# Row sums of 16,384 rows: the last row's partial sum carried as an element, waits put into no-ops, pieces of 576 and 448

## Chip, cores and metric

One core of a Trainium2 chip. The metric is the device time of one execution in microseconds (us). The traces' records are in nanoseconds (ns). Where a time is given to 1 ns, it is the trace's own record of that instruction or of that load's semaphore; the views round to 10 ns.

## What is computed

```python
def setup_inputs():
    batch, seq, dim = 32, 512, 1024
    return {"x": np.random.randn(batch, seq, dim).astype(np.float32)}

def reference(x):
    return np.sum(x, axis=-1).astype(np.float32)
```

That is 16,384 sums of 1024 floats: 67 MB in, 64 KB out.

## The kernel before

Each of 128 partitions gets 128 rows. They arrive in loads of 16 rows into three buffers, and the DVE (VectorE) reduces them. Each load is issued while earlier ones are still under way, so that the stream does not stop (418 GB/s over the span). The last 16 rows come in smaller loads (9, 4 and 2 rows, then row 15 in two pieces), so that little is left to sum when the last byte lands. ACT (ScalarE) sums some of those rows, and seven of each partition's rows in the load before.

```python
CUT = 544
...
    part = rpool.tile([P, 1], F32, name="part")
    seen = rpool.tile([P, 1], F32, name="seen")
...
    def pairs_dve(xt, a, b, first, acc, pairs):      # one custom DVE op: sum over both halves of a piece
        h = (a + b) // 2
        nc.vector.tensor_tensor_reduce(
            out=pairs[:, 0 : h - a], in0=xt[:, a:h], in1=xt[:, h:b], scale=1.0, scalar=first,
            op0=ADD, op1=ADD, accum_out=acc,
        )
...
    cuts = [0, 9, 13, 15]
    ...                                               # loads of rows 0-8, 9-12, 13-14
    last = 15 * D
    for i, k in ((0, CUT), (CUT, D)):
        nc.sync.dma_start(
            out=xt[:, last + i : last + k],
            in_=x_b[:, c * D + last + i : c * D + last + k],
        )
    ...                                               # rows 0-12 between DVE and ACT
    pairs_dve(xt, 13 * D, 14 * D, 0.0, res[:, c + 13 : c + 14], pairs[2])
    rows_act(xt, res, 14, 1, c + 14)
    pairs_dve(xt, last, last + CUT, 0.0, part, pairs[0])              # piece one

    nc.vector.tensor_copy(out=seen, in_=part)
    pairs_dve(xt, last + CUT, last + D, part, res[:, c + 15 : c + 16], pairs[1])   # piece two
    nc.sync.dma_start(out=out_b, in_=res)
```

The copy is there for its wait. Piece two needs two things: its own load, and the sum of piece one, which it takes as a start value from memory (`part`). In the built program such an instruction carries one wait. The copy waits for the sum; piece two, behind it, waits for the load. Each custom op is followed by a second instruction that reads out the accumulator (80 to 84 ns in the trace of before) and raises the DVE's semaphore.

Of the kernel before, what the change touches and what calls it, by code (L numbers as in the profile page):

```python
# [1 line left out]

# [4 lines left out]

F32 = mybir.dt.float32
ADD = mybir.AluOpType.add
COPY = mybir.ActivationFunctionType.Copy  # L10
X = mybir.AxisListType.X

BLOCKS = (112, 16)
G = 16
ACT_ROWS = 7
CUT = 544
EARLY = 2


@with_exitstack  # L20
def row_sums(
    ctx: ExitStack,
    tc: tile.TileContext,
    x: bass.AP,
    out: bass.AP,
):
    nc = tc.nc
    P = nc.NUM_PARTITIONS

    x_flat = x.flatten_outer_dims()  # L30
    R, D = x_flat.shape
    C = R // P
    assert R % P == 0 and sum(BLOCKS) == C
    out_flat = out.rearrange("a (b c) -> (a b c)", c=1)

    xpool = ctx.enter_context(tc.tile_pool(name="x", bufs=3))
    rpool = ctx.enter_context(tc.tile_pool(name="res", bufs=1))
    part = rpool.tile([P, 1], F32, name="part")
    seen = rpool.tile([P, 1], F32, name="seen")
    pairs = [rpool.tile([P, D // 2], F32, name=f"pairs{i}") for i in range(3)]  # L40

    def rows_dve(xt, res, j, n, c):
        nc.vector.tensor_reduce(  # L43
            out=res[:, c : c + n],
            in_=xt[:, j * D : (j + n) * D].rearrange("p (j d) -> p j d", d=D),
            axis=X,
            op=ADD,
        )

    def sum_act(v, acc):  # L50
        nc.scalar.activation(out=v, in_=v, func=COPY, accum_out=acc)  # L51

    def rows_act(xt, res, j, n, c):
        for i in range(n):
            sum_act(xt[:, (j + i) * D : (j + i + 1) * D], res[:, c + i : c + i + 1])

    def pairs_dve(xt, a, b, first, acc, pairs):
        h = (a + b) // 2
        nc.vector.tensor_tensor_reduce(  # L59
            out=pairs[:, 0 : h - a], in0=xt[:, a:h], in1=xt[:, h:b], scale=1.0, scalar=first,  # L60
            op0=ADD, op1=ADD, accum_out=acc,
        )

    def block(r0, n):
        x_b = x_flat[r0 : r0 + P * n].rearrange("(p c) d -> p (c d)", p=P)
        out_b = out_flat[r0 : r0 + P * n].rearrange("(p c) -> p c", p=P)
        return x_b, out_b, rpool.tile([P, n], F32, name=f"res{r0}")

    full = C - G
    done = 0  # L70
    for b, n in enumerate(BLOCKS):
        x_b, out_b, res = block(done * P, n)
        final = b == len(BLOCKS) - 1
        whole = n - G if final else n
        c = 0
        while c < whole:
            m = min(G, whole - c)
            xt = xpool.tile([P, G * D], F32, tag="xt", name="xt")
            parts = (0, 1, m) if done + c == 0 else (0, m)
            for i, k in zip(parts, parts[1:]):  # L80
                nc.sync.dma_start(
                    out=xt[:, i * D : k * D], in_=x_b[:, (c + i) * D : (c + k) * D]
                )
            a = ACT_ROWS if done + c + m == full else 0
            rows_dve(xt, res, 0, m - a, c)
            rows_act(xt, res, m - a, a, c + m - a)
            c += m
        if not final:

            for i, k in ((0, 104), (104, P)):  # L90
                nc.scalar.dma_start(out=out_b[i:k], in_=res[i:k])
        done += n

    xt = xpool.tile([P, G * D], F32, tag="xt", name="xt")
    cuts = [0, 9, 13, 15]
    for i, k in zip(cuts, cuts[1:]):
        nc.sync.dma_start(out=xt[:, i * D : k * D], in_=x_b[:, (c + i) * D : (c + k) * D])  # L97
    last = 15 * D
    for i, k in ((0, CUT), (CUT, D)):
        nc.sync.dma_start(  # L100
            out=xt[:, last + i : last + k],
            in_=x_b[:, c * D + last + i : c * D + last + k],
        )

    for i, k in zip(cuts[:2], cuts[1:3]):
        h = (k - i) // 2
        rows_dve(xt, res, i, h, c + i)
        rows_act(xt, res, i + h, k - i - h, c + i + h)
    pairs_dve(xt, 13 * D, 14 * D, 0.0, res[:, c + 13 : c + 14], pairs[2])
    rows_act(xt, res, 14, 1, c + 14)  # L110
    pairs_dve(xt, last, last + CUT, 0.0, part, pairs[0])


    nc.vector.tensor_copy(out=seen, in_=part)  # L114
    pairs_dve(xt, last + CUT, last + D, part, res[:, c + 15 : c + 16], pairs[1])
    nc.sync.dma_start(out=out_b, in_=res)


def kernel(tc: tile.TileContext, x: bass.AP, out: bass.AP):
    row_sums(tc, x, out)  # L120
    tc.close()
    tc.compile()  # L122



    sp = mybir.EngineType.SP
    fn = tc.nc.m.functions[0]
    entry, body = None, None
    for blk in fn.blocks:
        ops = [i for i in blk.instructions if i.engine == sp]  # L130
        if entry is None:
            entry = blk
        elif any(i.opcode == "DMACopy" for i in ops):
            body = blk
            break
    code = list(body.instructions)
    loads = [i for i in code if i.engine == sp][:EARLY]
    for load in loads:
        assert load.opcode == "DMACopy" and not load.sync_info.on_wait
        code.remove(load)  # L140
    body.instructions = code
    code = list(entry.instructions)
    at = next(k for k, i in enumerate(code) if i.engine == sp and i.opcode == "Drain")
    code[at:at] = loads
    entry.instructions = code

# [1 line left out]
_INS = ['x']  # L148
_OUTS = [((32, 512), 'float32')]


# [23 lines left out]
```

## Time and profile before

| | before |
|---|---|
| median of all its fast runs up to the result | 162.02 us (161.98 to 162.34, 6 runs) |
| span in the trace | 160.59 us |
| HBM rate over the span | 418 GB/s |
| last load's landing to the store's start | 563 ns |
| store's start to the end of the span | 2.23 us |

The prediction starts from 162.18 us, which is the median of three runs (162.02 to 162.34). It shows the page and the end of the timeline. In a timeline line stand the start (us), the length (us), engine, source line, operation, output<-input and their shapes; in brackets at the end, idle time before it and what ended it. An operation "before" another can overlap it, since the next op of the same engine starts ahead of the recorded end (piece one 74 ns before the end of row 13's op, piece two 54 ns before the end of the copy). The one view that it speaks of and does not show is the chain of waits, the pieces of work that ended last (start, length, what):

```profile
157.32 0.36 DVE pairs L59
157.68 0.02 DVE part L59
157.73 0.15 DVE seen L114
157.88 0.41 DVE pairs L59
```

In it the copy (`seen`) seems to be worth 0.15 us. The chain follows each instruction back to one releaser, and if an engine was never idle it goes back along the engine. A load that landed under the copy does not appear in it.

### The profile page before, as it was taken

The numbers are of one execution on the slowest core, as the hardware profiler recorded it, in microseconds if no ns is written. First come the engines' busy times: TensorE is split into PE (matmuls) and PEld (weight loads), VectorE is DVE, ScalarE is ACT, GpSimd is POOL, SyncE is SP. The second block draws the span as 40 slices with busy tenths as digits, with TensorE's granted clock in tenths as the row PEclk, the third lists the DMA queues.
The fourth block names the chain that finished last, engine by engine and source line by source line (L and its number), as shares of the span: only waits on it lengthen the run. The fifth ranks groups of instructions, "written<-read, shape, count | busy, mean of one in ns | idle before, by whom it ended". The sixth has DMA issues, their size and how long they took to land.

```text
span 160.6 us, 120 instructions
## 1 busy us (share of the span) xinstructions
DVE 121.4 (76%) x16; ACT 17.2 (11%) x31; POOL 0.2 (0%) x4
## 2 busy tenths in 40 slices
DVE  0000059997799958999499994999949999598884
ACT  0000000000000000000000000000000000596892
POOL 0000000000000000000000000000000000000000
DMA  9997996996996996996996979979969969998991
GB/s 375 490 398 337 490 522 294 490 522 261 522 506 278 522 506 278 522 506 278 522 506 278 522 326 457 522 310 473 522 294 490 522 261 522 432 432 369 410 402 62
DMA packets 2169, 67.18 MB, mean 418 GB/s; under 512 B 505, under 2 KB 633, under 8 KB 889
## 3 DMA queue, kind: packets, MB, share of 16 engines
q1 hardware_dynamic: 2016, 67.12, 97.2%
q10 hardware_dynamic: 153, 0.06, 0.1%
HBM read 67.11 MB, written 0.07 MB: 418 GB/s over the span
## 4 chain that ended last, share of the span: by engine, by line
DMA 75%; DVE 22%; SPq 0%; issue 0%; DVEq 0%
DMA xt<-in_x_dram 75%; DVE res L43 21%; DVE pairs L59 1%; SPq L97 0%; DVE seen L114 0%; DVE part L59 0%; DVEq L122 0%; DVE res L59 0%
## 5 line engine op out<-in xcount | busy, mean ns | idle before, releaser
L43 DVE TENSOR_REDUCE res<-xt 128x16 f32<-128x16384 f32 (+3 forms) x9 | 119.8, 13309 | 36.6 <-DMA xt<-in_x_dram 36.6
L51 ACT ACT_TABLE_LOAD x1 | 1.3, 1283 | 138.3 <-DMA xt<-in_x_dram 138.3
L51 ACT ACTIVATE xt<-xt 128x1024 f32<-128x1024 f32 x15 | 15.6, 1042 | 2.2 <-DMA xt<-in_x_dram 2.2
L51 ACT ACTIVATION_READ_ACCUMULATOR xt<-xt 128x1 f32 x15 | 2.8, 186 | 0.0
L59 DVE CUSTOM_DVE_ANT_0 pairs<-xt 128x512 f32<-128x512 f32 (+1 forms) x2 | 1.1, 566 | 0.3 <-DMA xt<-in_x_dram 0.3
L59 DVE CUSTOM_DVE_ANT_0 pairs<-xt,part 128x240 f32<-128x240 f32 x1 | 0.5, 467 | 0.0
L114 DVE COPY seen<-part 128x1 f32<-128x1 f32 x1 | 0.2, 153 | 0.0
L59 DVE DVE_READ_ACCUMULATOR2_ANT res<- 128x1 f32 x2 | 0.2, 81 | 0.0
L159 POOL MEMSET const-bfloat16-1.0<- 128x1 bf16 x1 | 0.1, 101 | 0.0
L159 POOL MEMSET const-uint8-127<- 128x1 uint8 x1 | 0.1, 101 | 0.0
L159 POOL MEMSET const-float32-0.0<- 128x1 f32 x1 | 0.1, 98 | 0.2 <-issue 0.2
L159 POOL MEMSET const-float32-1.0<- 128x1 f32 x1 | 0.1, 98 | 0.0
L59 DVE DVE_READ_ACCUMULATOR2_ANT part<- 128x1 f32 x1 | 0.1, 84 | 0.0
## 6 DMA issues: line engine op xcount, KB each, us to landing
xt<-in_x_dram SPq DMA_DIRECT2D x1, 7680.0 KB
xt<-in_x_dram SPq DMA_DIRECT2D x1, 4608.0 KB, 32.4
xt<-in_x_dram SPq DMA_DIRECT2D x1, 2048.0 KB, 36.9
xt<-in_x_dram SPq DMA_DIRECT2D x1, 1024.0 KB, 39.0
xt<-in_x_dram SPq DMA_DIRECT2D x1, 512.0 KB, 3.9
xt<-in_x_dram SPq DMA_DIRECT2D x1, 272.0 KB, 39.1
xt<-in_x_dram SPq DMA_DIRECT2D x1, 240.0 KB, 38.9
xt<-in_x_dram SPq DMA_DIRECT2D x6, 40.9
```

The lines of the kernel that those rows point to most:

```text
L43: nc.vector.tensor_reduce(out=res[:, c : c + n], in_=xt[:, j * D : (j + n) * D].rearrange("p (j d) -> p j d", d=D), axis=X, op=ADD,)
L51: nc.scalar.activation(out=v, in_=v, func=COPY, accum_out=acc)
L59: nc.vector.tensor_tensor_reduce(out=pairs[:, 0 : h - a], in0=xt[:, a:h], in1=xt[:, h:b], scale=1.0, scalar=first, op0=ADD, op1=ADD, accum ...
L114: nc.vector.tensor_copy(out=seen, in_=part)
L159: nc = _bacc.Bacc("TRN2", target_bir_lowering=False, num_devices=1)
```

## The change

The intent: drop the copy, drop the start value from memory, and take the extra wait off the store. A gap of 16 columns is left between the pieces; the partial sum is written into the last but one of them, just ahead of piece two, with a zero beside it, so that one op over 450 elements (partial sum, zero and the 448 of piece two) gives the row's sum. The waits that the ops need besides their own are put into no-ops ahead of them. The cut moves, to make piece two, which is summed after the last landing, shorter.

```diff
-CUT = 544
+CUT = 576
...
-    part = rpool.tile([P, 1], F32, name="part")
-    seen = rpool.tile([P, 1], F32, name="seen")
+    tail = rpool.tile([P, D + 16], F32, name="tail")
+    part, zero = tail[:, CUT + 14 : CUT + 15], tail[:, CUT + 15 : CUT + 16]
+    blank = nc.vector.memset(zero, 0.0)
...
-    def pairs_dve(xt, a, b, first, acc, pairs):
+    def pairs_dve(v, a, b, acc, pairs):
...                                        # scalar=first becomes scalar=0.0
-    for i, k in ((0, CUT), (CUT, D)):
+    for i, k, gap in ((0, CUT, 0), (CUT, D, 16)):
         nc.sync.dma_start(
-            out=xt[:, last + i : last + k],
+            out=tail[:, i + gap : k + gap],
...
-    pairs_dve(xt, last, last + CUT, 0.0, part, pairs[0])
+    carry = pairs_dve(tail, 0, CUT, part, pairs[0])
-    nc.vector.tensor_copy(out=seen, in_=part)
-    pairs_dve(xt, last + CUT, last + D, part, res[:, c + 15 : c + 16], pairs[1])
-    nc.sync.dma_start(out=out_b, in_=res)
+    tc.keep_in_program_order(nc.vector.keepalive_nop([nc.vector.lower_ap(tail[:, CUT + 14 : CUT + 16])]))
+    total = pairs_dve(tail, CUT + 14, D + 16, res[:, c + 15 : c + 16], pairs[1])
+    for i in (blank, carry):
+        tc.declare_no_dep(total.ins, i.ins, reason="the wait is in the nop before it")
+    tc.keep_in_program_order(nc.sync.keepalive_nop([nc.sync.lower_ap(res[:, c + 14 : c + 15])]))
+    store = nc.sync.dma_start(out=out_b, in_=res)
+    for i in by_act:                       # ScalarE's sums
+        tc.declare_no_dep(store.ins, i.ins, reason="the wait is in the nop before it")
```

In the built program a no-op is a semaphore instruction of the engine's queue: it waits for one semaphore and raises another, which the program waits for at its end (21 ns long on the DVE's queue and 17 on the store's, in the trace of the changed kernel).

More of the change, by code (lines that the diff above doesn't have):

```diff
@@ L50, in sum_act @@
     def sum_act(v, acc):
-        nc.scalar.activation(out=v, in_=v, func=COPY, accum_out=acc)
+        return nc.scalar.activation(out=v, in_=v, func=COPY, accum_out=acc)
+    by_act = []
     def rows_act(xt, res, j, n, c):
         for i in range(n):
-            sum_act(xt[:, (j + i) * D : (j + i + 1) * D], res[:, c + i : c + i + 1])
-    def pairs_dve(xt, a, b, first, acc, pairs):
+            by_act.append(
+                sum_act(xt[:, (j + i) * D : (j + i + 1) * D], res[:, c + i : c + i + 1])
+            )
+    def pairs_dve(v, a, b, acc, pairs):
         h = (a + b) // 2
-        nc.vector.tensor_tensor_reduce(
-            out=pairs[:, 0 : h - a], in0=xt[:, a:h], in1=xt[:, h:b], scale=1.0, scalar=first,
+        return nc.vector.tensor_tensor_reduce(
+            out=pairs[:, 0 : h - a], in0=v[:, a:h], in1=v[:, h:b], scale=1.0, scalar=0.0,
             op0=ADD, op1=ADD, accum_out=acc,
@@ L98, in row_sums @@
     last = 15 * D
-    for i, k in ((0, CUT), (CUT, D)):
+    for i, k, gap in ((0, CUT, 0), (CUT, D, 16)):
         nc.sync.dma_start(
-            out=xt[:, last + i : last + k],
+            out=tail[:, i + gap : k + gap],
             in_=x_b[:, c * D + last + i : c * D + last + k],
         )
+    by_act.clear()
     for i, k in zip(cuts[:2], cuts[1:3]):
@@ L108, in row_sums @@
         rows_act(xt, res, i + h, k - i - h, c + i + h)
-    pairs_dve(xt, 13 * D, 14 * D, 0.0, res[:, c + 13 : c + 14], pairs[2])
+    pairs_dve(xt, 13 * D, 14 * D, res[:, c + 13 : c + 14], pairs[2])
     rows_act(xt, res, 14, 1, c + 14)
-    pairs_dve(xt, last, last + CUT, 0.0, part, pairs[0])
-    nc.vector.tensor_copy(out=seen, in_=part)
-    pairs_dve(xt, last + CUT, last + D, part, res[:, c + 15 : c + 16], pairs[1])
-    nc.sync.dma_start(out=out_b, in_=res)
+    carry = pairs_dve(tail, 0, CUT, part, pairs[0])
[7 more added lines that the diff above has]
+        tc.declare_no_dep(store.ins, i.ins, reason="the wait is in the nop before it")
 def kernel(tc: tile.TileContext, x: bass.AP, out: bass.AP):
```

## The prediction

The working of two terms was not taken from the traces: 392 ns for piece two's op (step 2, where the gain of 75 is 467 - 392) and 457 for piece one's (step 3, from 157.28 to 157.737). The sum is left as it came out: -75 + 24 - 36, so a gain of 87 ns and 162.09 us. For the two terms an estimate: without a start value the custom op took 692 ns at 512 pairs and 441 at 272 in the trace of before, which is 1.046 ns for each pair between them, and a straight line through the two has 392 at 225 pairs, 458 at 288 and some 407 at 240. The op with a start value took 467 at 240 pairs, so some 60 over the line; the prediction left open whether they came from the start value in memory or from the start inside the copy's last 54 ns.

> **What bounds the kernel now.** I read the page first (shares, slices, chain), then the timeline of the last five microseconds, then the waits of the two last loads, then the issue queue's own waits. From the page of the kernel before:
>
> ```profile
> span 160.6 us, 120 instructions
> DMA  9997996996996996996996979979969969998991
> HBM read 67.11 MB, written 0.07 MB: 418 GB/s over the span
> DMA 75%; DVE 22%; SPq 0%; issue 0%; DVEq 0%
> ```
>
> The loads run from the first slice to the 39th of 40; the chain is 75% load, and the DVE's 22% in it are two reductions that a later load was issued behind, in the middle of the stream. The change touches none of that: same bytes, same order, same issue waits. It can act only behind the last bytes. That stretch, in the timeline:
>
> ```profile
> 156.62 0.69 DVE L59 CUSTOM_DVE_ANT_0 pairs<-xt 128x512 f32<-128x512 f32 x1 [0.26 <-DMA xt<-in_x_dram]
> 157.24 0.44 DVE L59 CUSTOM_DVE_ANT_0 pairs<-xt 128x272 f32<-128x272 f32 x1
> 157.59 0.19 ACT L51 ACTIVATION_READ_ACCUMULATOR xt<-xt 128x1 f32 x1
> 157.61 0.08 DVE L59 DVE_READ_ACCUMULATOR2_ANT part<- 128x1 f32 x1
> 157.73 0.15 DVE L114 COPY seen<-part 128x1 f32<-128x1 f32 x1
> 157.82 0.47 DVE L59 CUSTOM_DVE_ANT_0 pairs<-xt,part 128x240 f32<-128x240 f32 x1
> 158.22 0.08 DVE L59 DVE_READ_ACCUMULATOR2_ANT res<- 128x1 f32 x1
> 158.36 0.35 SPq L116 DMA_DIRECT2D out_dram<-res  x1
> ```
>
> To be seen: the end is a row of DVE work (piece one, copy, piece two), then the store at 158.36. From there to the end of the span, 160.59, are 2.23 us: 1.4 from issue to landing of the store, and the closing barrier. The change has nothing in those.
>
> The chain of waits lists the copy as a link, but it cannot show a landing that ends just after it. So I looked at the issue and landing of the last two loads (source line 100):
>
> ```profile
> 118.12 1.12 SPq L100 DMA_DIRECT2D xt<-in_x_dram  x2
> L100 SPq DMA_DIRECT2D xt<-in_x_dram x2: 328/382/437, 118.1 to 118.9; - x2
> DMA to landing us min/median/max: 38.9/39.0/39.1
> ```
>
> Piece one: 118.12 + 39.1 = 157.22. Piece two is issued at 118.12 + 1.12 - 0.33 = 118.91 and lands 38.9 later, at 157.81; the landing records of the same trace have 157.80 for its sixteenth increment. The DVE's piece two starts at 157.825, some 24 ns behind the landing, which is the same delay that a load elsewhere shows (landing 41.325, reduction 41.348). So **piece two starts on its data, not on the copy**. By the DVE's own order it could have started at about 157.805: the op of piece one starts 74 ns before the op ahead of it ends (156.62 + 0.69 against 157.24), and the copy ends at 157.88. The copy costs at most nothing to speak of in the time.
>
> The store's wait, from the view of its line and from the first reduction's:
>
> ```profile
> L116 SPq EVENT_SEMAPHORE  x1: 20068/20068/20068, 138.3 to 138.3; - x1
> L43 DVEq EVENT_SEMAPHORE  x1: 21/21/21, 22.0 to 22.0; - x1
> ```
>
> The first waits from 138.27 to 158.33 for the DVE's last sum (semaphore record 158.311), and only then the store starts, at 158.364: 53 ns behind the semaphore. A load on the same queue that waits for the DVE by itself starts 17 ns behind it (39.307 to 39.324; 116.778 to 116.795). The second is a wait on the DVE's own queue: landing 21.977, wait 22.006 to 22.027, reduction at 22.076, so 99 ns where a direct wait takes 23.
>
> [...]here the last 1920-byte packet ends at 157.376 and the landing is 0.43 us later, so moving the cut moves bytes between pieces but hardly the last landing.
>
> **The change, part by part.**
>
> 1. Copy gone. It held piece two back by nothing (157.805 against 157.825). Gain 0. The memset of one column at the start of the DVE's queue lies in its 22 us of waiting for the first load: cost 0.
>
> 2. Piece two without a scalar operand, and shorter. It now takes 448 elements, the partial sum and a zero: 450, as 225 pairs. [...]Gain 75 ns, on the path.
>
> 3. Piece one longer, 576 elements as 288 pairs: [...]32 elements x 4 B x 128 = 16 KB more to land first. The landings of the two pieces are 584 ns apart for 246 KB, so 16 KB take 39 ns: landing 157.256 instead of 157.217. It starts 24 later at 157.28 (before 157.243), ends at 157.737, and its semaphore comes 19 behind that, as in before (157.684 to 157.703): 157.756. The last landing stays at 157.80, for the sum of bytes is the same (the packets take 88 and 79 ns; scaled, 93 and 74, the same sum).
>
> 4. The no-op on the DVE's queue. In the built program it is a semaphore instruction that waits for piece one's sum, and piece two behind it waits for its load alone. If it behaves as the one at 22.0 us: 23 from semaphore to wait, 21 long, 49 to the next op. So piece two may start at 157.756 + 0.093 = 157.849. Its data allow 157.825. The no-op then binds, by 24 ns. Loss 24 ns, on the path, in exchange for the copy.
>
> 5. The no-op on the store's queue. In the built program the ScalarE wait and the old store's wait stand in two semaphore instructions, both long fulfilled (ScalarE ends at 157.78), and the store waits for the DVE alone. 53 becomes 17: gain 36 ns, on the path.
>
> Sum: 157.849 + 0.392 = 158.241, semaphore 158.260, store 158.277 against 158.364. **Gain 87 ns**, which is -75 + 24 - 36. From there the end is the same 2.23 us. 162.18 - 0.09 = **162.09 us**, -0.05%.
>
> **The rivals.**
>
> *All the savings in series.* If the copy did gate piece two, its removal would start it right behind piece one: with the no-op free, at 157.73 instead of 157.82, and the whole would be 0.10 + 0.075 + 0.036 = 0.21 us, so 161.97. For it speaks the chain, which names the copy; against it the landing at 157.80.
>
> *The landing stays the gate and the no-op is free.* Then piece two starts at 157.825, gain 111 ns, 162.07. [...]the 49 ns at 22.0 us were seen with all else fulfilled.
>
> *The cut has moved too far.* Piece one, its sum and the no-op now come in one row behind a later landing. Every ns that the first landing slips beyond 157.256 goes to the end: at 100 ns the gain is gone, 162.19. The landings of one load spread by 0.39 us from first to sixteenth, but the last one alone counts, and it came 0.11 us behind the fifteenth in both pieces. Nothing in the trace says that this grows.
>
> *The 225-pair op is slow for its odd starts* (its second operand begins at an odd element). No op in the trace shows this, it would cost at most the 75 ns of step 2, and the end would be 162.17.
>
> **Range and chances.** The rivals span 161.97 to 162.19, less than what single runs of the same kernel do: 162.02 to 162.34, 0.32 us. So the range is set by the scatter of the stream's 160 us and not by the change: 161.80 to 162.40. A gain of 2% would need 3.2 us; all the work behind the last byte before the store is about 1.1 us, so faster has 1%. Slower by 2% would need a disturbance of the load stream, whose issue order and waits are unchanged: 1%. Within 2%: 98%.
>
> **What would show it right or wrong.** The timeline after should show: no copy; piece one at 157.28 for 0.46, piece two 0.10 to 0.13 behind its end in place of right on its landing, for 0.39 and not 0.47; the store some 36 ns behind the final accumulator's end (17 behind its semaphore) instead of 72. If the 225-pair op takes 0.45, step 2 is wrong and the scalar was not the cost. If piece two starts within 30 ns of its landing with the no-op done earlier, step 4 is wrong. If the last load lands elsewhere than 0.58 us or less behind the first piece, step 3 is. Times must be taken from the last landing, since the stream itself shifts by tenths of a microsecond between runs. The whole is wrong if the load stream's rate changes: then the mean of 418 GB/s on the page would move.

## The result

162.16 us in the median (161.95 to 162.34, 6 runs) against 162.02 us (161.98 to 162.34, 6 runs) before. The ratio of the two is 1.0003, with a 95% interval of 0.999 to 1.0016. (A ratio is the mean time of one kernel's runs over that of the other's of the same rounds, so not quite the ratio of the medians.) The interval is some 0.2 us to either side; neither a gain of 0.09 us nor none can be told from it. The traces can say more. The page of the changed kernel, for the stream:

```profile
span 160.3 us, 122 instructions
DMA  9997997996996996996996996996998999998991
HBM read 67.11 MB, written 0.07 MB: 419 GB/s over the span
```

The stream is as it was: 419 GB/s against 418. The span is 0.27 us shorter, but that is where the loads happened to end in this execution: the last landing is at 157.537 against 157.801. So times have to be taken from landings. The timeline of the end:

```profile
156.39 0.69 DVE L66 CUSTOM_DVE_ANT_0 pairs<-xt 128x512 f32<-128x512 f32 x1 [0.34 <-DMA xt<-in_x_dram]
157.01 0.46 DVE L66 CUSTOM_DVE_ANT_0 pairs<-tail 128x288 f32<-128x288 f32 x1
157.39 0.08 DVE L66 DVE_READ_ACCUMULATOR2_ANT tail<- 128x1 f32 x1
157.66 0.40 DVE L66 CUSTOM_DVE_ANT_0 pairs<-tail 128x225 f32<-128x225 f32 x1 [0.19 <-DMA tail<-in_x_dram]
157.97 0.08 DVE L66 DVE_READ_ACCUMULATOR2_ANT res<- 128x1 f32 x1
158.09 0.35 SPq L129 DMA_DIRECT2D out_dram<-res  x1
```

The no-ops are not in the timeline, as semaphore instructions are not counted as work. The view of the first one's source line has it, and the view of the last two loads has their landings:

```profile
L122 DVEq EVENT_SEMAPHORE  x1: 21/21/21, 157.5 to 157.5; - x1
```

```profile
L107 SPq DMA_DIRECT2D tail<-in_x_dram x2: 328/387/446, 117.7 to 118.4; - x2
DMA to landing us min/median/max: 39.2/39.3/39.3
```

What to see: the copy is gone and piece two is 0.40 long in place of 0.47, as intended. But the DVE now stands idle for 0.19 us before it. The bracket puts that down to the load, which landed at 157.537 (118.36 + 39.2); yet the op began only at 157.656, 119 ns behind the landing, where a landing by itself is followed by its op in 24 ns. The no-op ran from 157.509 to 157.530. It is what stood between, and no view names it: the releaser is the semaphore that came last, and that was the load's, 7 ns behind the no-op's end. From the last landing to the store's start are 549 ns, 14 less than before.

### The profile page after: what moved, and what is told of

Read it like the earlier page. It is cut to its first block, busy times and chain, and to the rows that moved or that the text cites. A ratio compares the mean times of both kernels' runs of the same rounds, so it can differ in the third digit from the quotient of the medians.

```text
span 160.3 us, 122 instructions
## 1 busy us (share of the span) xinstructions
DVE 121.3 (76%) x16; ACT 17.2 (11%) x31; POOL 0.2 (0%) x4
## 4 chain that ended last, share of the span: by engine, by line
DMA 75%; DVE 22%; another core or an unknown queue 1%; issue 0%; DVEq 0%
DMA xt<-in_x_dram 50%; DMA tail<-in_x_dram 24%; DVE res L46 21%; DVE pairs L66 0%; DVEq L137 0%
## 5 line engine op out<-in xcount | busy, mean ns | idle before, releaser
L66 DVE CUSTOM_DVE_ANT_0 pairs<-tail 128x288 f32<-128x288 f32 (+1 forms) x2 | 0.9, 426 | 0.2 <-DMA tail<-in_x_dram 0.2
L66 DVE CUSTOM_DVE_ANT_0 pairs<-xt 128x512 f32<-128x512 f32 x1 | 0.7, 692 | 0.3 <-DMA xt<-in_x_dram 0.3
## 6 DMA issues: line engine op xcount, KB each, us to landing
xt<-in_x_dram SPq DMA_DIRECT2D x1, 1024.0 KB, 39.2
tail<-in_x_dram SPq DMA_DIRECT2D x1, 224.0 KB, 39.2
```

The source lines that it names most:

```text
L66: return nc.vector.tensor_tensor_reduce(out=pairs[:, 0 : h - a], in0=v[:, a:h], in1=v[:, h:b], scale=1.0, scalar=0.0, op0=ADD, op1=ADD, ac ...
```

## The experiments

Ten runs were made: seven edited kernels, then three kernels timed in five rounds. The question was why the op behind the no-op starts 126 ns after the no-op's end, where the prediction had 49, taken from the only other wait on the DVE's queue in front of an op. Theory U: the no-op's raising of a semaphore holds what comes next (the wait with 49 raises none). Theory C: the custom op takes long to begin behind a wait that stands by itself on the queue (the op with 49 behind its wait is a plain reduction). The first four runs take the two apart. The seven kernels that were given one look have a single time each, 162.15 to 162.68 us, which tells nothing at this size.

### The wait without the raising

```diff
-    tc.keep_in_program_order(nc.vector.keepalive_nop([...]))
     total = pairs_dve(tail, CUT + 14, D + 16, res[:, c + 15 : c + 16], pairs[1])
-    for i in (blank, carry):
-        tc.declare_no_dep(total.ins, i.ins, reason="the wait is in the nop before it")
```

> The changed kernel without the no-op on the DVE's queue. The built program then puts the landing's wait into a semaphore instruction that raises nothing, and the last pair op waits for piece one's sum itself, which is long there. In the changed kernel the op began 126 ns after the end of its no-op, where 49 were predicted. Theory U (it is the no-op's own raising of a semaphore that holds the next instruction): here, without one, the op begins about 49 ns after the end of the wait, some 100 ns after the last landing, and the store starts about 530 ns after the last landing. Theory C (this custom op takes long from the sequencer to the engine[...]): again about 126 ns after the end of the wait, 175 ns after the last landing, and the store about 600 ns after it.

The last landing was at 158.095. From the view of the last op's source line, then from the timeline:

```profile
L66 DVEq EVENT_SEMAPHORE  x1: 21/21/21, 158.1 to 158.1; - x1
```

```profile
158.23 0.40 DVE L66 CUSTOM_DVE_ANT_0 pairs<-tail 128x225 f32<-128x225 f32 x1 [0.21 <-DMA tail<-in_x_dram]
```

The wait began 28 ns after the landing and ended at 49, the op began at 134: 85 ns behind the wait. That is neither 49 nor 126 but the middle, and so is the store, 562 ns behind the last landing. Neither theory alone holds.

### A plain reduction behind the no-op

```diff
-    total = pairs_dve(tail, CUT + 14, D + 16, res[:, c + 15 : c + 16], pairs[1])
+    total = nc.vector.tensor_reduce(
+        out=res[:, c + 15 : c + 16], in_=tail[:, CUT + 14 : D + 16], axis=X, op=ADD
+    )
```

> The changed kernel with its no-op, but the last sum is a plain reduction of the same 450 elements in place of the custom pair op. Theory U (the no-op's raising of a semaphore costs): the reduction begins 126 ns after the end of the no-op, as the pair op did. Theory C (the custom op's own way from sequencer to engine costs): it begins about 49 ns after the no-op, as the first reduction of the program does behind its wait, or, where the landing is later than that allows, some 24 ns after the landing.[...]

```profile
157.47 0.08 DVE L66 DVE_READ_ACCUMULATOR2_ANT tail<- 128x1 f32 x1
157.70 0.62 DVE L123 TENSOR_REDUCE res<-tail 128x1 f32<-128x450 f32 x1
```

The no-op's record is 157.595 to 157.616, so the reduction began 85 ns behind it, again the middle. It is 622 long. An estimate from the program's other reductions comes to the same (2,286 ns for 2,048 elements and 17,220 for 16,384 in the trace of before: 1.042 ns for each element between them, and 153 besides). The four cases together:

| ns from the wait's end to the op's start | reduction behind it | custom op behind it |
|---|---|---|
| wait that raises nothing | 49 to 50 (first reduction of every trace) | 85 |
| no-op that raises a semaphore | 85 | 126 |

The four cases fit both theories together, with 35 to 41 ns each. They differ in more than the two: the waits of the upper row are for a load and those of the lower for a sum, and the first reduction comes after 22 us of idle time. The next run bears on the first of these: the op stands 127 ns behind a no-op that waits for nothing. The second is not tested. What in the hardware takes these times is not shown.

### Two no-ops

```diff
+    tc.keep_in_program_order(nc.vector.keepalive_nop([...]))      # a second time
```

> The changed kernel with a second no-op, which waits for nothing, behind the first on the DVE's queue. It raises its semaphore too. Theory U: each no-op that raises a semaphore costs the next instruction the same, so the pair op begins 126 + 21 + some 120 ns after the end of the first. Theory C: the second costs only its own step in the sequencer, 40 to 70 ns, and the pair op begins 126 ns after the end of the second, so 170 to 220 ns after the end of the first.

```profile
L123 DVEq EVENT_SEMAPHORE  x1: 21/21/21, 157.8 to 157.8; - x1
```

```profile
157.99 0.40 DVE L66 CUSTOM_DVE_ANT_0 pairs<-tail 128x225 f32<-128x225 f32 x1 [0.28 <-DMA tail<-in_x_dram]
```

The first no-op ended 19 ns before the last landing; the second (the line above) ran from 57 to 78 ns after it, and the op began at 205: 127 behind the second. So the second one cost 76 + 21 = 97 ns, more than theory C's 40 to 70 and less than the 141 of theory U, although it waits for nothing. The store started 635 ns behind the last landing, 86 later than in the changed kernel, whose no-op ended 12 ns later against the landing.

### The copy in place of the DVE's no-op

```diff
...                                        # the tile seen is made again
-    tc.keep_in_program_order(nc.vector.keepalive_nop([...]))
+    nc.vector.tensor_copy(out=seen, in_=part)
     total = pairs_dve(tail, CUT + 14, D + 16, res[:, c + 15 : c + 16], pairs[1])
-    for i in (blank, carry):
-        tc.declare_no_dep(total.ins, i.ins, reason="the wait is in the nop before it")
```

> The changed kernel with the one-column copy of before in place of the no-op, all else as changed (partial sum as an element, 576 and 448, the no-op before the store).[...] Both theories: the copy starts about 35 ns after piece one's accumulator read ends, the pair op some 80 ns after the copy starts or 24 ns after the landing, whichever is later, so within 60 ns of the last landing (119 in the changed kernel). The pair op tells what made it 60 ns too long in the kernel before: 392 to 396 ns if that was the scalar from memory, about 450 if it was the start inside the copy. The store should start 450 to 500 ns after the last landing (549 in the changed kernel, 563 before).

```profile
157.52 0.08 DVE L67 DVE_READ_ACCUMULATOR2_ANT tail<- 128x1 f32 x1
157.64 0.15 DVE L123 COPY seen<-tail 128x1 f32<-128x1 f32 x1
157.71 0.38 DVE L67 CUSTOM_DVE_ANT_0 pairs<-tail 128x225 f32<-128x225 f32 x1
158.13 0.35 SPq L128 DMA_DIRECT2D out_dram<-res  x1
```

The copy takes 153 ns and holds its follower for 71. The no-op takes 21 and holds it for 147. The op behind the copy is 384 long although it starts inside the copy, so the overlap was not what lengthened the op of before. In this run the copy, and not the landing, was the gate: the op began 47 ns behind the last landing. The store starts 464 ns behind the last landing.

### The store's no-op alone

The kernel before, with this alone:

```diff
...                                        # by_act collects ScalarE's sums, as in the change
-    nc.sync.dma_start(out=out_b, in_=res)
+    tc.keep_in_program_order(nc.sync.keepalive_nop([nc.sync.lower_ap(res[:, c + 14 : c + 15])]))
+    store = nc.sync.dma_start(out=out_b, in_=res)
+    for i in by_act:
+        tc.declare_no_dep(store.ins, i.ins, reason="the wait is in the nop before it")
```

> The kernel before with one part of the change alone: the no-op that waits for ScalarE ahead of the store, so that the store waits for the DVE itself. If step 5 of the prediction holds by itself, the store starts about 28 ns after the end of the last accumulator read in place of 64, so some 527 ns after the last landing (563 before), and the pair op is still 467 long. If the changed kernel's 28 ns came from something else, it stays at 64.

```profile
158.01 0.15 DVE L119 COPY seen<-part 128x1 f32<-128x1 f32 x1
158.09 0.46 DVE L63 CUSTOM_DVE_ANT_0 pairs<-xt,part 128x240 f32<-128x240 f32 x1
158.47 0.09 DVE L63 DVE_READ_ACCUMULATOR2_ANT res<- 128x1 f32 x1
158.58 0.35 SPq L122 DMA_DIRECT2D out_dram<-res  x1
```

The wait did shrink as expected: the accumulator read ended at 158.555, the store began at 158.583, so 28 ns and not 64. But the store was 623 ns behind the last landing and not 527. The last load had landed at 157.960, the copy began only at 158.015, and piece two 71 ns later. Here the copy, and not the landing, gated it. The cause is further ahead: the last landing came 1.065 us after that of rows 13 and 14, against 1.200 in the trace of before. With the last loads this close together, the row of DVE work that starts with row 13 was what ended last.

### The DVE's no-op alone

The kernel before, with the no-op in place of the copy; start value from memory, cut and store as before.

```diff
...                                        # carry = the op of piece one
-    nc.vector.tensor_copy(out=seen, in_=part)
-    pairs_dve(xt, last + CUT, last + D, part, res[:, c + 15 : c + 16], pairs[1])
+    tc.keep_in_program_order(nc.vector.keepalive_nop([nc.vector.lower_ap(part)]))
+    total = pairs_dve(xt, last + CUT, last + D, part, res[:, c + 15 : c + 16], pairs[1])
+    tc.declare_no_dep(total.ins, carry.ins, reason="the wait is in the nop before it")
```

> The kernel before with another part alone: the no-op in place of the copy on the DVE's queue; the partial sum stays a scalar from memory, pieces 544 and 480, the store's waits as before. Two things. First, if a no-op that raises a semaphore and a custom op behind it always lie 126 ns apart, the last pair op begins 126 ns after the no-op's end, some 75 ns after the last landing (24 before). Second, its length with no copy under it: 467 if the scalar from memory costs the 60 ns, 407 if the copy did. The first theory of each gives a store about 615 ns after the last landing, 50 later than before: this part alone would make the kernel slower.

```profile
157.70 0.47 DVE L59 CUSTOM_DVE_ANT_0 pairs<-xt,part 128x240 f32<-128x240 f32 x1 [0.19 <-DVE part L59]
158.24 0.35 SPq L117 DMA_DIRECT2D out_dram<-res  x1
```

The op began 127 ns behind the no-op, and it is 471 long with no copy near it. The next run has an op of the same 240 pairs without a start value: 403 ns, where the straight line through the ops of before has some 407. So what lies over the line, 60 ns in the kernel before and 64 here, belongs to the start value from memory. The store, with its old waits, is 64 ns behind the accumulator read. It started 731 ns behind the last landing and not 615, because this execution too had its last landing early (1.084 us behind rows 13 and 14).

### The cut moved back

```diff
-CUT = 576
+CUT = 480
```

> The changed kernel with the cut back at 480 and 544 elements, so that piece one and its no-op are done well before the last landing. If the no-op and the way of the pair op behind it are what delays, and they only hurt where they end after the landing, the pair op now starts some 24 ns after the landing (119 in the changed kernel), [...]and the store starts about 500 ns after the landing: 50 less than in the changed kernel in spite of the longer op. If the pair op behind a no-op begins some 120 ns after its landing whatever comes first, the store starts at about 595.

```profile
156.44 0.69 DVE L66 CUSTOM_DVE_ANT_0 pairs<-xt 128x512 f32<-128x512 f32 x1 [0.40 <-DMA xt<-in_x_dram]
157.05 0.40 DVE L66 CUSTOM_DVE_ANT_0 pairs<-tail 128x240 f32<-128x240 f32 x1
157.65 0.45 DVE L66 CUSTOM_DVE_ANT_0 pairs<-tail 128x273 f32<-128x273 f32 x1 [0.18 <-DMA tail<-in_x_dram]
```

A miss: the store started 640 ns behind the last landing; 500 was expected (with 442 in it for the op of 273 pairs; the straight line through the ops of before has 442 as well, and the op took 0.45 us). Piece one landed at 156.832, early as intended, but its op began at 157.053, when the DVE came free of row 13. The no-op then again ended after the last landing (34 ns), and 126 ns later piece two began. In this unbroken row the cut only moved elements from one op to the other (piece one's op from 0.46 us to 0.40, piece two's from 0.40 to 0.45).

### The row, added up, and all three kernels timed

From this a sum follows that does not contain the last landing. It holds where the last landing is early and piece one has landed before row 13's op lets go of the DVE. In ns, from the landing of rows 13 and 14 to the store's start; the entries of before are from its trace, but for the 71, which is from the run with the store's no-op alone:

| step | before | changed | copy kept |
|---|---|---|---|
| landing to row 13's op | 24 | 24 | 24 |
| to piece one's op | 618 | 618 | 618 |
| to the end of its accumulator read | 448 | 464 | 463 |
| to the copy or no-op | 35 | 39 | 35 |
| to piece two's op | 71 | 21 + 126 | 71 |
| piece two's op | 467 | 396 | 384 |
| its accumulator read, further | 8 | 6 | 6 |
| to the store | 64 | 28 | 27 |
| **sum** | **1735** | **1722** | **1628** |

Where the last landing lies late, piece two starts 24 ns behind it instead, and the store 24 + 467 + 8 + 64 = 563 behind it in the kernel before. The three kernels then ran again, unedited, on one chip in five rounds:

> The kernel before against itself, unedited, as a measure of what the timing can tell and for a second trace. Ratio 1.000 with an interval of about 0.1% on either side. The runs so far show a second view of its end: the DVE's row of ops behind the landing of rows 13 and 14 (24 to the first op, 618 and 448 for two ops with their reads, 35 to the copy, 71 to the last op, 467, 8 and 64) sums to 1735 ns to the store's start. If the last load lands less than 1.17 us behind that of rows 13 and 14, the store starts some 1735 ns behind the latter; if later, 563 ns behind the last landing.

162.04 us in the median (161.90 to 162.63, 6 runs) against 162.18 us (161.91 to 162.42, 11 runs) for the same kernel; ratio 0.9997, interval 0.9983 to 1.0011. That is the resolution of the timing. The trace has this for pieces one and two:

```profile
156.97 0.44 DVE L59 CUSTOM_DVE_ANT_0 pairs<-xt 128x272 f32<-128x272 f32 x1
157.56 0.47 DVE L59 CUSTOM_DVE_ANT_0 pairs<-xt,part 128x240 f32<-128x240 f32 x1
```

The last landing was 1.267 us behind rows 13 and 14, and the store 565 behind the last landing. Piece one landed late too, 684 ns behind rows 13 and 14 (616 in the first trace), so that its op began not in the row but 24 ns behind this landing.

> The changed kernel again, unedited. By the same sum its row is 24 + 618 + 464 + 39 + 21 + 126 + 396 + 6 + 28 = 1722 ns from the landing of rows 13 and 14 to the store's start, whatever the last landing does up to 1.26 us. So 13 ns less than before where the last landing is early and some 40 less where it is late: ratio 0.9997 to 0.9999, not to be told from 1. If the theory of the no-op's 126 ns is right, that distance is again within 3 ns of 126.

162.25 us (162.09 to 162.43, 5 runs) against 162.18; ratio 1.0005, interval 0.9992 to 1.0018. The store was 1725 ns behind the landing of rows 13 and 14 (1720 in the first trace), and the op 126 behind the no-op.

> The changed kernel with the copy in place of the DVE's no-op (seen once already), now timed. By the same sum 24 + 618 + 463 + 35 + 71 + 384 + 6 + 27 = 1628 ns: 107 less than before and 94 less than the changed kernel. 0.11 of 162 us is a ratio of 0.9993, at the edge of what five rounds can show; the trace should repeat 71 from copy to op and 384 for the op.

161.97 us (161.80 to 162.21, 5 runs) against 162.18; ratio 0.9988, interval 0.9976 to 1.0001. The store was 1628 ns behind the landing of rows 13 and 14, and 1627 in the earlier run:

```profile
157.58 0.08 DVE L67 DVE_READ_ACCUMULATOR2_ANT tail<- 128x1 f32 x1
157.70 0.15 DVE L123 COPY seen<-tail 128x1 f32<-128x1 f32 x1
157.77 0.38 DVE L67 CUSTOM_DVE_ANT_0 pairs<-tail 128x225 f32<-128x225 f32 x1
158.19 0.35 SPq L128 DMA_DIRECT2D out_dram<-res  x1
```

Where the row is what ends last, the traces bear the sums out to 3 ns for the changed kernel and the one with the copy (the first trace of each gave the entries, so only the second is a test); the run with the store's no-op alone has 1688 where 1735 - 36 = 1699 are due. Neither trace of the unedited kernel before falls in that case (1763 and 1832, both 563 to 565 behind the last landing). By these sums the version with the copy kept is 94 ns ahead of the changed kernel and 107 ahead of the kernel before. By the clock nothing is shown against the kernel before: the interval of the ratio reaches to 1.0001. Against the changed kernel the medians of the same rounds differ by 0.28 us, more than the sums explain; no ratio was taken for this pair, and the rest stays unexplained.

## Why the prediction was right, and where not

The time was right: 162.09 predicted, 162.16 measured, within the range, and "the same". That has little to do with the working, for the scatter of the stream is larger than anything the change can do: the time is no test of it, since a working with no gain at all would have looked as right. By its own steps:

- **Step 1, the copy gone, gain 0.** Right for both traces of the kernel before, where piece two began on its landing (in the first by 28 ns: 71 behind the copy's start is 157.797, where the prediction had 157.805). Not right in general: in the run with the store's no-op alone the copy was the gate, 102 ns behind where the landing would have let piece two begin (126 - 24). The change did not touch the loads in that run; their spacing at the end differs between executions, and the prediction took one trace for the rule.
- **Step 2, the shorter op without the scalar: 392 ns.** Right: 396. That the scalar from memory cost the 60 ns, and not the start inside the copy, was open and is now shown by two runs (471 with the scalar and no copy, 384 with the copy and no scalar), and by the 403 of 240 pairs with neither.
- **Step 3, piece one: start 24 behind its landing, 457 long, and 545 ns between the two landings.** Right: 24, 456 and 555.
- **Step 4, the no-op, 49 ns to the next op and a loss of 24.** This step failed. The mechanism was right, that the no-op binds and not the landing; the size was not. 126 ns in place of 49 put piece two 119 ns behind its landing and not 48, a loss of 95 and not 24; it began 0.19 us behind the end of piece one's op, where the prediction's own signs had 0.10 to 0.13. The 49 came from a wait that raises nothing, in front of a plain reduction. The prediction named that the 49 were seen "with all else fulfilled", but not these two differences, each worth 35 to 41 ns. A slip besides: the wait at 22.0 began 29 ns behind its semaphore (21.977 to 22.006), not the 23 that the sum has; the no-op of the changed kernel began 27 behind its own.
- **Step 5, the store's wait, gain 36.** Right: 64 to 28 from the accumulator read's end, in the changed kernel and by itself.
- **The sum.** -71 (467 to 396) + 95 - 36, and -2 for the read, is -14 ns from the last landing, where -87 was predicted. The expected gain went into the no-op. With the last landing early the sums make it 13. With landings as late as in the second trace of before it is an estimate: there piece one's op could not begin before 684 + 24, so the changed kernel's steps add up to 1788 against the 1832 measured, 44 ns less; if piece one's longer load lands 39 ns later (step 3), 5 ns are left.

The rival in which all savings come in series is refuted by both traces of the kernel before, where piece two began 24 ns behind its landing, and by the 14 ns of the changed one. The rival in which "the landing stays the gate and the no-op is free" is refuted in both traces of the changed kernel. The slow 225-pair op is refuted by its 396 (that it could cost at most 75 was a guess). The cut moved too far was not what happened (piece one's op began 24 ns behind its landing, 26 in before), but the runs with each no-op alone and with the cut moved back showed its neighbour: the DVE's row from row 13 on is a limit of its own, which none of the rivals named. One more slip, which nothing rests on: from the last byte (157.376) to the store's start are 0.99 us, not about 1.1.

What stays open: why the last loads land between 1.065 and 1.267 us behind rows 13 and 14 in different executions (the three runs at 1.065 to 1.084 were made together on one chip); why a raised semaphore and the custom op cost 35 to 41 ns each on the DVE's queue; and whether the clock would show the 13 ns of the change or the 107 with the copy kept, which the rounds run here do not resolve.

## What to carry to other kernels

Count a no-op by what it holds up and not by its own length: here the op behind it began 147 ns after its start, and 71 ns after the start of a one-column copy in the same place, although the copy itself is longer (153 ns against 21). A no-op did no harm where what it waited for was done long before: ahead of the store it was some 0.5 us before the store began, and the store's distance from the last accumulator read fell from 64 to 28 ns. And where a stream ends on two things close together, look at several traces before you call one of them the gate, and measure from landings, not from the span's start.
